# A prologue written out operation by operation: modulation quarters between the first projections

## The chip, the cores and the metric

One core of a Trainium2 chip runs the kernel; all its work is one program on five engines: TensorE (PE, its weight loads PEld), VectorE (DVE), ScalarE (ACT), GpSimd (POOL) and SyncE (SP, which issues loads). Each engine works through its own list of instructions in the order in which the program was written, and waits at an instruction until what it needs is there. The metric is the device time of one execution in microseconds (us), as the median over several runs.

## What is computed

Two layers of a backbone; each layer modulates and normalises its 1024 latent and 256 context tokens, projects them with `w_in`, mixes three groups of heads, gates and projects back. The prologue of layer 0, which the change rewrites, is this part of the reference (x stands for latent, ctx for context tokens):

```python
shift, scale, gate = jnp.split(jax.nn.silu(c) @ w_mod + b_mod, 3, axis=-1)
shift_c, scale_c, gate_c = jnp.split(jax.nn.silu(c_ctx) @ w_mod + b_mod, 3, axis=-1)
h = rms_norm(x, norm_g) * (1 + scale[:, None]) + shift[:, None]
hc = rms_norm(ctx, norm_g) * (1 + scale_c) + shift_c
p = h @ w_in          # layer 0 also: pc = hc @ w_in
```

## The kernel before, in words

Everything is float32. A projection takes three matmuls in place of one: the modulated activations and the weights are each split into a high half (rounded to the type that the fast matmul takes) and a low half (the rest), and high by high, low by high and high by low are added up in PSUM.

In the prologue of layer 0 these pieces occur:

- **Modulation quarters** q = 0 to 3. Shift and scale for the 1024 features are computed by quarters of 256 features; a quarter's weights are four loads of 512 KB (`mod0_load`). `mod0_mm` multiplies them on PE (8 matmuls, 16 records in the trace since each float32 matmul is two). `mod0_fin` turns the two result rows into columns: DVE copies them (L162), PE transposes four pieces (L166), and `mod_finish` makes shift and scale of them on DVE (L136 to L141). Quarter q serves the feature blocks k = 2q and 2q + 1.
- **Token tiles** j = 0 to 9, 128 tokens each: 0 to 3 are group g = 0, 4 to 7 are g = 1, the context tiles 8 and 9 are g = 2. A tile is loaded (L256), squared and summed on ACT in two halves (L266), its factor is computed on POOL (L267 to L269), and DVE multiplies the tile by it (L575).
- **A block (k, g)**, `h_block`: PE transposes feature block k of the group's tiles (L280), DVE (L286) or ACT (L284) applies scale and shift, ACT makes the high half (L287), POOL makes the low half, for g = 2 DVE (L289).
- **Gate matmuls** of (k, g): `proj_T_k` (L340), six matmuls on the block's two halves, for two column tiles of the first `w_in` chunk, which `w_split` has split (L317, L318).

Before, the order is this: loads of quarters 0 to 2, of the first `w_in` chunk, of all ten tiles, then of quarter 3 and the next chunk. PE computes quarters 0, 1 and 2 one after another. Then a loop goes over `items`: blocks k = 0 to 5 of g = 0, of g = 1, of g = 2, then the blocks of k = 6 and 7; the gate matmuls of an item come three items behind its block. Quarter 3 isn't computed on PE but on DVE: `mod0_acc` adds up 32 products (L176, L178) between items 8 and 15, and `mod0_sum` sums them over partitions with 16 small matmuls (L187). SP keeps a number of loads in flight and issues the next as an earlier one arrives. Behind the prologue come the Fourier matrices (L384) and the next projections.

Of the kernel before, what the change touches and what calls it, by code (L numbers as in the profile page):

```python
# [31 lines left out]
def build(tc, I, out):  # L32
# [127 lines left out]
    def mod0_fin(q, pm):  # L160
        row = E2()
        dve.tensor_copy(row[0:2, :], pm[0:2, :])  # L162
        ps = PX()
# [109 lines left out]
    def h_block(l, k, g, xn, H, on_act=False):  # L273
        tiles = GROUPS[g]
        s = 1 if g == 2 else 0
        n = 128 * len(tiles)
        c0 = tiles[0] * 128
        ps = PX()
        for i, j in enumerate(tiles):
            pe.transpose(ps[:, i * 128:i * 128 + 128], xn[j][:, k * 128:k * 128 + 128], ident)  # L280
# [251 lines left out]
    def layer(l, src, dst, carry):  # L532
# [27 lines left out]
        if full:  # L560
# [31 lines left out]
            W = wready.pop(0)  # L592
            a3 = T5([128, 4, 256])
            psg = [[PX() for _ in cols(ntokA)] for _ in range(2)]
            items = [(k, g) for g in (0, 1, 2) for k in range(6)] + [(k, g) for k in (6, 7) for g in (0, 1, 2)]
            at = {n: [] for n in range(len(items))}
            at[0] += [lambda: rms(0, 1, 2, 3), lambda: norm(0, 1), lambda: mod0_fin(2, ms[2]), lambda: norm(2, 3)]
            for n, j in enumerate((4, 5, 6, 7, 8, 9)):
                at[n] += [lambda j=j: rms(j)]
                at[n + 1] += [lambda j=j: norm(j)]  # L600
            for n in range(8, 16):
                at[n] += [lambda: next(acc)]
            at[18] += [lambda: mod0_sum(3, a3)]
            for n in range(len(items) + 3):
                if n < len(items):
                    for f in at[n]:
                        f()
                    hb(*items[n], 6 <= n < 17)
                if n == 0:
                    w3 = mod0_load(3)  # L610
                    acc = mod0_acc(w3, a3)
                    w_dma()
                if n >= 3:
                    gk(*items[n - 3])
                if n == 20:
                    dve.tensor_copy(identR, ident)
                    pool.tensor_scalar(pscT, pscT, 0.5, 0.0, MULT, ADD)
                    tabs = fourier_tabs(l)
                    css = [fourier_load(l, ct) for ct in range(2)]
                if n == 22:  # L620
                    w_split()
                    w_dma()
# [729 lines left out]
```

## Time and profile before

| | us |
|---|---|
| median of 3 runs | 1448.14 |
| lowest, highest | 1446.84, 1451.79 |
| the profiled execution's own time | 1448.99 |
| its span, first to last instruction | 1447.0 |
| PE busy | 1381.8 (95%) |
| DVE busy | 979.2 (68%) |
| POOL busy | 775.9 (54%) |
| ACT busy | 567.6 (39%) |

The profile is of one execution. An engine's busy share is a mean over stages that have different limits; what a rewritten prologue is worth is read from the prologue's own stretch, by when PE leaves it, and from whether PE has idle time behind it.

### The profile page before, as it was taken

To read this page: it belongs to the slowest core of one execution; us is meant where nothing else is said; L and a number is where in the kernel's file an instruction comes from. 1 tells how busy PE (TensorE), PEld (TensorE's weight loads), DVE (VectorE), ACT (ScalarE), POOL (GpSimd) and SP (SyncE) were. 2 spreads that over 40 slices of the span, in tenths; PEclk is the share of its full clock that TensorE was granted. 3 is DMA by queue.
4 is the path that set the end of the run, shared out by engine and by line. 5 is a ranking of instruction groups with operands and counts; after the bars stand their busy time and mean duration, and the time that the engine had idled before them with its cause. 6 is when DMAs were issued, how large, how long until landed. Compare 5 with 4: busy or idle time off the path is not lost.

```text
span 1447.0 us, 24063 instructions
## 1 busy us (share of the span) xinstructions
PE 1381.8 (95%) x9364; PEld 1240.6 (86%) x9364; DVE 979.2 (68%) x1553; ACT 567.6 (39%) x1230; POOL 775.9 (54%) x827
## 2 busy tenths in 40 slices
PE   7899999899999998999999899999999999999998
PEld 1688899779999987888888778988999998888887
DVE  2853366886895178798898654573464319989896
ACT  2632212101232265666665433121131227656663
POOL 2543222456785057667677842226887107766664
PEclk9899999999999999999999999999999999999999
DMA  9220242575123032112113321526412202111110
GB/s 354 101 90 32 85 149 91 187 266 166 60 88 117 1 103 81 66 45 74 45 45 112 104 66 38 205 80 213 148 44 85 78 22 67 45 45 45 59 59 30
DMA packets 65153, 137.07 MB, mean 95 GB/s; under 512 B 7312, under 2 KB 19728, under 8 KB 65040
## 3 DMA queue, kind: packets, MB, share of 16 engines
q1 hardware_dynamic: 49712, 108.82, 22.5%
q10 hardware_dynamic: 15328, 26.72, 5.3%
q8 instruction: 74, 1.21, 0.3%
q14 instruction: 39, 0.32, 0.1%
HBM read 105.63 MB, written 29.88 MB: 94 GB/s over the span
## 4 chain that ended last, share of the span: by engine, by line
PE 46%; DVE 21%; POOL 7%; issue 3%; ACT 2%; DMA 2%; ACTq 0%; POOLq 0%; SPq 0%; DVEq 0%
PE x L360 16%; DVE sm L923 6%; PE S L913 6%; PE x L1056 6%; PE x L993 5%; PE x L340 5%; PE x L753 3%; DVE e L1020 3%; PE x L977 2%; DVE t L952 1%; DVE t L980 1%; POOL e L759 1%; POOL sm L803 1%; DVE t L210 1%; PE x L892 1%
## 5 line engine op out<-in xcount | busy, mean ns | idle before, releaser
L360 PE MATMUL x<-wh,t 128*128 128x256 f32 x2432 | 445.9, 285 | 0.1
L360 PEld LDWEIGHTS x<-wh,t 128*128 128x128 f32 x2432 | 381.7, 192 | 1.8 <-issue 1.0
L360 PE MATMUL x<-wl,t 128*128 128x256 f32 x1216 | 344.7, 283 | 0.0
L923 DVE TENSOR_REDUCE sm<-S 128x1 f32<-128x1280 f32 (+1 forms) x132 | 194.8, 1476 | 72.2 <-PE S L913 72.0
L360 PEld LDWEIGHTS x<-wl,t 128*128 128x128 f32 x1216 | 233.7, 192 | 1.3 <-issue 1.2
L913 PE MATMUL S<-t,e 128*128 128x512 f32 (+1 forms) x768 | 180.9, 371 | 2.8 <-ACT e L899 1.4
L340 PE MATMUL x<-t,wh 128*128 128x512 f32 (+1 forms) x640 | 173.3, 381 | 8.8 <-DVE t L289 4.3
L938 ACT ACTIVATE t<-S,sm 128x1280 f32<-128x1280 f32 (+1 forms) x140 | 171.7, 1230 | 1.2 <-DVE sm L923 1.2
L993 PE MATMUL x<-t,t 128*128 128x128 f32 x1312 | 157.5, 275 | 3.3 <-DVE t L980 2.7
L993 PEld LDWEIGHTS x<-t,t 128*128 128x128 f32 x1312 | 153.7, 192 | 6.4 <-DVE t L980 2.9
L913 PEld LDWEIGHTS S<-t,e 128*128 128x128 f32 x768 | 126.3, 190 | 20.6 <-ACT t L938 2.0
L340 PEld LDWEIGHTS x<-t,wh 128*128 128x128 f32 x640 | 114.1, 192 | 31.6 <-POOL t L289 5.4
L318 POOL TENSOR_TENSOR wl<-st,wh 128x1024 fp32r<-128x1024 f32 x36 | 93.1, 2587 | 84.3 <-ACT wh L317 83.6
L961 POOL TENSOR_TENSOR t<-t,t 128x768 f32<-128x768 f32 (+1 forms) x64 | 116.2, 1816 | 5.3
L317 ACT ACTIVATE wh<-st 128x1024 fp32r<-128x1024 f32 x64 | 64.8, 1059 | 138.4 <-DMA xpart<-e 45.8
L977 PE MATMUL x<-ident,t 128*128 128x128 f32 x636 | 101.2, 274 | 5.7 <-DVE e L1059 4.1
L953 POOL TENSOR_SCALAR t<-t,sm 128x768 f32<-128x768 f32 x62 | 83.4, 1344 | 42.8 <-DVE sm L949 26.6
L753 PE MATMUL x<-wh,t 128*128 128x512 f32 x288 | 93.6, 404 | 8.5 <-DVE t L528 4.7
L1056 PE MATMUL x<-wh,e 128*128 128x512 f32 (+1 forms) x312 | 98.9, 384 | 2.6 <-ACT e L899 1.0
L340 PE MATMUL x<-t,wl 128*128 128x512 f32 (+1 forms) x320 | 100.2, 374 | 0.0
L210 DVE SCALAR_TENSOR_TENSOR t<-t,sc,t 128x512 f32<-128x512 f32 x98 | 90.8, 968 | 1.5 <-DMA t<-in_wmB_dram 1.1
L977 PEld LDWEIGHTS x<-ident,t 128*128 128x128 f32 x636 | 75.1, 141 | 15.9 <-DVE e L1059 4.5
(224 smaller groups left out, 2318.0 us busy)
## 6 DMA issues: line engine op xcount, KB each, us to landing
st<-in_w_in_dram SPq DMA_DIRECT2D x48, 512.0 KB, 4.0
t<-in_wmB_dram ACTq DMA_DIRECT2D x24, 512.0 KB, 5.4
xpart<-e ACTq DMA_DIRECT2D x36, 256.0 KB, 3.8
t<-xpart SPq DMA_DIRECT2D x18, 512.0 KB, 3.9
t<-in_wmS_dram SPq DMA_DIRECT2D x16, 512.0 KB, 8.5
st<-in_w_out_dram SPq DMA_DIRECT2D x16, 512.0 KB, 5.1
t<-in_x_dram SPq DMA_DIRECT2D x10, 512.0 KB, 10.3
e<-in_x_dram SPq DMA_DIRECT2D x20, 256.0 KB, 4.5
```

The lines of the kernel that those rows point to most:

```text
L210: dve.scalar_tensor_tensor(a, w, sk, a, MULT, ADD)
L318: lo_eng[hf].tensor_tensor(lo[:, sl, :], st, hi[:, sl, :].bitcast(F32), SUB)
L340: pe.matmul(p[:, :m], lhsT=W[wi][:, k, ct * 128:ct * 128 + 128], rhs=H[k][hi][:, c0:c0 + m], start=(n == 0), stop=(n == 3 * KT - 1))
L360: pe.matmul(bank[:, i * 256:i * 256 + 256], lhsT=H[k][hi][:, j * 128:j * 128 + 128], rhs=W[wi][:, k, :], start=(n == 0), stop=(n == 3 * KT ...
L753: pe.matmul(ps, lhsT=zr[k][zi][:, j * 128:j * 128 + 128], rhs=W[wi][:, k, :], start=(n == 0), stop=(n == 11))
L913: pe.matmul(S[:, i * nk + c:i * nk + c + n], lhsT=s["qT"][i][:, m * 2 + f, :], rhs=kT[2 * h + m][:, k0 + c:k0 + c + n], start=(f == 0), st ...
L923: dve.tensor_reduce(nb, S[:, :nh * nk].rearrange("p (h k) -> p h k", h=nh), AX.X, ALU.min)
L938: act.activation(p[:, sl], S[:, sl], AF.Exp, bias=nb[:, i:i + 1], scale=-1.0, accum_out=ls[:, i:i + 1])
L961: pool.tensor_tensor(p[0][:, cut:end], p[0][:, cut:end], p[1][:, cut:end], ADD)
L977: pe.transpose(ps[:, i * 128:i * 128 + 128], s["p"][0][:, (t0 + i) * 128:(t0 + i + 1) * 128], ident)
L993: pe.matmul(o[:, i * 128:i * 128 + 128], lhsT=s["PT"][:, i * nkt + t, :], rhs=vv[h][:, kt0 + t, :], start=(t == 0), stop=(t == nkt - 1))
L1056: pe.matmul(ps[:, :m], lhsT=zz[:, k, :], rhs=Wa[hf][wi][:, k, w0:w0 + m], start=(n == 0), stop=(n == 11))
```

## The change

The loop over items is replaced by a written list of operations: `m` computes a quarter on PE, `f` turns it, `n` squares, sums and multiplies a tile, `t` transposes a block, `s` splits it, `g` does its gate matmuls. All four quarters are computed on PE; `mod0_acc` and `mod0_sum` are gone. `h_block` is cut in two, `h_trans` and `h_split`. The two small operations of a tile's factor move from POOL to DVE, its power stays on POOL. The loads come in the order quarter 0, x0 to x3, the chunk of `w_in`, quarter 1, x4 to x7, quarter 2, x8 and x9, quarter 3. The context's gate matmuls (`g02` to `g72`) all come last.

```diff
-    def mod0_acc(ws, acc):
-        for k in range(KT):
-            for i in range(2):
...
-    def mod0_sum(q, acc):
...
+    def h_trans(k, g, xn):
+        ps = PX()
+        for i, j in enumerate(GROUPS[g]):
+            pe.transpose(ps[:, i * 128:i * 128 + 128], xn[j][:, k * 128:k * 128 + 128], ident)
+        return ps
...
             def rms(*js):
                 for j in js:
                     rx[j] = SM(1)
-                    for _ in x_rms(xn[j], rx[j]):
-                        pass
+                    ss = SM(2)
+                    for hf in range(2):
+                        sq = E2()
+                        act.activation(sq, xn[j][:, hf * 512:hf * 512 + 512], AF.Square, accum_out=ss[:, hf:hf + 1])
+                    dve.tensor_tensor(rx[j], ss[:, 0:1], ss[:, 1:2], ADD)
+                    dve.tensor_scalar(rx[j], rx[j], 1.0 / D, EPS, MULT, ADD)
+                    pool.tensor_tensor(rx[j], rx[j], mhalf[:, 0:1], ALU.pow)
...
+            def run(op, *a):
+                if op == "m":
+                    mods[a[0]] = mod0_mm(wm[a[0]])
+                elif op == "f":
+                    mod0_fin(a[0], mods[a[0]])
+                elif op == "n":
+                    rms(*a)
+                    norm(*a)
+                elif op == "t":
+                    banks[a] = h_trans(*a, xn)
+                elif op == "s":
+                    newH(a[0])
+                    h_split(l, *a, banks[a], H, a[0] >= 4 and a[1] == 1)
+                elif op == "g":
...
+            wm = [mod0_load(0)]
+            x_in(0, 1, 2, 3)
             w_dma()
-            x_in(0, 1, 2, 3, 4, 5, 6, 7, 8, 9)
-            ms = [mod0_mm(wm[0])]
-            ms.append(mod0_mm(wm[1], lambda: mod0_fin(0, ms[0])))
-            ms.append(mod0_mm(wm[2], lambda: mod0_fin(1, ms[1])))
-            w_split()
...
+            wm.append(mod0_load(1))
+            x_in(4, 5, 6, 7)
+            wm.append(mod0_load(2))
+            x_in(8, 9)
+            wm.append(mod0_load(3))
+
+            for text in (
+                    "m0 n0 n1 f0 n2 n3 t00 t10 s00 t20 s10 W t30 m1 g00 f1 g10 s20 s30 n4 n5 n6 n7 g20 g30",
+                    "t01 t11 s01 t21 s11 t31 s21 g01 s31 g11 m2 g21 f2 g31 t40 t50 s40 n8 n9 t41 s50 t51 s41 g40 s51 g50",
+                    "t02 t12 s02 g41 s12 g51 t22 t32 s22 s32 m3 t42 f3 t52 s42 s52 X t60 t70 s60 s70 t61 s61 g60",
+                    "t71 s71 g70 Y t62 t72 g61 s62 s72 g71 g02 g12 g22 g32 g42 g52 g62 g72"):
```

`W` splits the first chunk of weights and issues the next, `X` makes small constants and issues the Fourier tables' loads, `Y` splits the second chunk. Behind the prologue the order of the instructions is the same on every engine.

What the list does to the engines' queues shows at three places. The first is PE's queue around the first transposes of token tiles (tiles `t_17` and on, into `x_297`). Before (x_200 is quarter 2's result, L166 the turning):

```order
L157 MATMUL x_200<-t_12_140,sc 2x512 x2
L166 MATMUL x_207<-ident,e_33_205 128x2 x4
L157 MATMUL x_200<-t_13_142,sc 2x512 x2
L157 MATMUL x_200<-t_14_144,sc 2x512 x2
L166 MATMUL x_274<-ident,e_61_272 128x2 x4
L280 MATMUL x_297<-ident,t_17_150 128x128
```

and after, where quarter 1 (into `x_281`) follows the last transposes of group 0 (block 3, into `x_276`), and the first gate matmuls (into `x_290`) follow it:

```order
L252 MATMUL x_276<-ident,t_9_134 128x128
L252 MATMUL x_276<-ident,t_10_136 128x128
L155 MATMUL x_281<-t_13_142,sc 2x512 x2
L155 MATMUL x_281<-t_14_144,sc 2x512 x2
L155 MATMUL x_281<-t_15_146,sc 2x512 x2
L155 MATMUL x_281<-t_16_148,sc 2x512 x2
L321 MATMUL x_290<-t_53_249,wh_266 128x512
L321 MATMUL x_290<-t_54_250,wh_266 128x512
L321 MATMUL x_290<-t_53_249,wl_267 128x512
```

Quarters 1 to 3, of which two stood ahead of every transpose of a tile, now stand between them.

The second place is ACT's queue at the squares of the tiles of group 1. Before, the squares (L266, of `t_21` and `t_22`, tiles 4 and 5) stand around the high half of block (0, 0), `t_68`:

```order
L266 ACTIVATE e_59_263,sm_262<-t_20_156 128x512
L266 ACTIVATE e_60_265,sm_262<-t_20_156 128x512
L266 ACTIVATE e_66_288,sm_287<-t_21_158 128x512
L266 ACTIVATE e_67_290,sm_287<-t_21_158 128x512
L287 ACTIVATE t_68_295<-e_71_302 128x512
L266 ACTIVATE e_80_321,sm_320<-t_22_160 128x512
```

and after, the tiles 4 and 5 are `t_17` and `t_18`, and `t_71` and `t_74` are the high halves of blocks (2, 0) and (3, 0), which use quarter 1:

```order
L298 ACTIVATE wh_266<-st_140 128x1024
L265 ACTIVATE t_71_316<-e_73_318 128x512
L265 ACTIVATE t_74_322<-e_76_324 128x512
L554 ACTIVATE e_79_330,sm_329<-t_17_150 128x512
L554 ACTIVATE e_80_332,sm_329<-t_17_150 128x512
L554 ACTIVATE e_83_340,sm_339<-t_18_152 128x512
```

The squares of tiles 4 and on have moved behind four high halves and the split of the weights.

The third place is DVE's queue at the context tiles. Before, tiles 8 and 9 (`t_25`, `t_26`) are multiplied between the scalings (L286) of group 0, and the products of quarter 3 (L176) follow:

```order
L286 TENSOR_SCALAR e_109_404<-x_399,scaleT_99,shiftT_97 128x512
L575 TENSOR_SCALAR t_25_166<-t_25_166,sm_388 128x1024
L286 TENSOR_SCALAR e_117_431<-x_426,scaleT_99,shiftT_97 128x512
L575 TENSOR_SCALAR t_26_168<-t_26_168,sm_415 128x1024
L176 TENSOR_SCALAR t_38_227<-t_72_306,sc 128x256 x4
```

and after, they stand between the scalings of blocks (4, 0) and (5, 0) (`e_111`, `e_123`), behind the end of quarter 2 (L141):

```order
L141 TENSOR_TENSOR scaleT_99<-sm_453,ngT 128x4
L264 TENSOR_SCALAR e_111_475<-x_463,scaleT_99,shiftT_97 128x512
L555 TENSOR_TENSOR sm_479<-sm_480 128x1
L556 TENSOR_SCALAR sm_479<-sm_479 128x1
L561 TENSOR_SCALAR t_25_166<-t_25_166,sm_479 128x1024
L555 TENSOR_TENSOR sm_489<-sm_490 128x1
L556 TENSOR_SCALAR sm_489<-sm_489 128x1
L561 TENSOR_SCALAR t_26_168<-t_26_168,sm_489 128x1024
L264 TENSOR_SCALAR e_123_506<-x_468,scaleT_99,shiftT_97 128x512
```

The two tiles' six operations have moved in front of the scaling of block (5, 0); the products of quarter 3 are gone.

## Rows read from the trace of the kernel before

**Rows 1.** The page's head and its first part: busy time (share of the span) and instructions.

```profile
span 1447.0 us, 24063 instructions
PE 1381.8 (95%) x9364; PEld 1240.6 (86%) x9364; DVE 979.2 (68%) x1553; ACT 567.6 (39%) x1230; POOL 775.9 (54%) x827
```

**Rows 2.** Busy time of the engines in stretches of the prologue and behind it: from:to and length in us, then busy us (instructions) of PE, PEld, DVE, ACT, POOL, the granted clock as a share of 2.4 GHz, the DMA engines' busy share, GB/s.

```profile
0.00:15.60 15.60, 9.67 (x18) 1.77 (x19) 0.98 (x5) 1.70 (x3) 0.19 (x4) 1.00 0.85 286
15.60:38.10 22.50, 17.99 (x59) 6.28 (x58) 10.71 (x23) 9.90 (x26) 9.92 (x17) 0.91 1.04 404
38.10:64.40 26.30, 23.68 (x115) 18.23 (x113) 20.99 (x25) 19.39 (x41) 21.04 (x27) 0.94 0.24 89
64.40:72.20 7.80, 4.70 (x25) 4.16 (x23) 7.80 (x21) 1.96 (x4) 0.00 (x0) 0.75 0.25 70
72.20:92.40 20.20, 17.64 (x99) 15.78 (x98) 11.84 (x21) 7.01 (x18) 8.70 (x6) 0.84 0.33 106
92.40:250.00 157.60, 157.58 (x1005) 141.08 (x1006) 82.98 (x145) 37.55 (x67) 45.22 (x28) 1.00 0.25 83
```

**Rows 3.** PE's waits from 0 to 92 us: who waited for what, us in total, times, longest.

```profile
PE x L157 <- DMA t<-in_wmS_dram: 5.9, 1, 5.9
PE x L340 <- DVE t L289: 4.3, 3, 2.4
PE x L166 <- DVE e L162: 3.2, 1, 3.2
PE x L280 <- DVE t L575: 2.4, 3, 1.1
```

**Rows 4.** PE's timeline from 0 to 38.2 us: start, us, then line, operation, out<-in, shapes, count, and the idle time before with what ended it.

```profile
5.93 12.61 PE L157 MATMUL x<-t,sc 128*2 128x512 f32 x24 [5.93 <-DMA t<-in_wmS_dram]
18.47 0.40 PE L166 MATMUL x<-ident,e 2*128 2x2 f32 x4
18.80 7.03 PE L157 MATMUL x<-t,sc 128*2 128x512 f32 x16
...
26.10 3.60 PE L157 MATMUL x<-t,sc 128*2 128x512 f32 x8
32.92 0.41 PE L166 MATMUL x<-ident,e 2*128 2x2 f32 x4 [3.23 <-DVE e L162]
...
35.45 3.04 PE L280 MATMUL x<-ident,t 128*128 128x128 f32 x13 [0.18 <-DVE t L575]
38.14 1.50 PE L340 MATMUL x<-t,wh 128*128 128x512 f32 x2
```

**Rows 5.** PE's timeline, the starts of two items of latent tiles in a row, of a context item and of the item behind it, and the prologue's end.

```profile
41.09 0.60 PE L280 MATMUL x<-ident,t 128*128 128x128 f32 x4
...
42.92 0.60 PE L280 MATMUL x<-ident,t 128*128 128x128 f32 x4
...
83.84 0.38 PE L280 MATMUL x<-ident,t 128*128 128x128 f32 x2
...
84.77 0.63 PE L340 MATMUL x<-t,wh 128*128 128x512 f32 x2
...
90.42 1.06 PE L384 MATMUL x<-e 128*128 128x128 f32 x8
```

**Rows 6.** SP's timeline: the issues of the ten tile loads.

```profile
15.14 12.21 SPq L256 DMA_DIRECT2D t<-in_x_dram  x10
```

**Rows 7.** ACT's timeline: the squares of tile 0 and the start of tile 1.

```profile
25.75 0.63 ACT L266 ACTIVATE e<-t 128x512 f32<-128x512 f32 x1 [0.23 <-DMA t<-in_x_dram]
...
27.04 0.63 ACT L266 ACTIVATE e<-t 128x512 f32<-128x512 f32 x1
```

**Rows 8.** DVE's timeline (and one row of POOL's): the copy of quarter 0, its four small operations, POOL's power for tile 0 and DVE's multiplication of that tile.

```profile
15.15 0.68 DVE L162 COPY e<-x 2x512 f32<-2x512 f32 x1 [11.78 <-PE x L157]
18.91 0.16 DVE L136 TENSOR_TENSOR shiftT<-x,bmodT 128x4 f32<-128x4 f32 x1 [3.09 <-PE x L166]
18.99 0.15 DVE L139 TENSOR_TENSOR sm<-x,bmodT 128x4 f32<-128x4 f32 x1
19.18 0.17 DVE L140 TENSOR_SCALAR sm<-sm 128x4 f32<-128x4 f32 x1
19.38 0.16 DVE L141 TENSOR_TENSOR scaleT<-sm,ngT 128x4 f32<-128x4 f32 x1
...
29.46 0.56 POOL L269 TENSOR_TENSOR sm<-sm,mhalf 128x1 f32<-128x1 f32 x1
...
30.05 0.75 DVE L575 TENSOR_SCALAR t<-t,sm 128x1024 f32<-128x1024 f32 x1 [0.72 <-POOL sm L269]
```

**Rows 9.** The split of block (0, 0) on DVE, ACT and POOL.

```profile
35.97 0.81 DVE L286 TENSOR_SCALAR e<-x,scaleT,shiftT 128x512 f32<-128x512 f32 x1 [0.57 <-PE x L280]
...
36.81 0.63 ACT L287 ACTIVATE t<-e 128x512 fp32r<-128x512 f32 x1 [4.54 <-DVE e L286]
...
37.52 1.27 POOL L289 TENSOR_TENSOR t<-e,t 128x512 fp32r<-128x512 f32 x1 [1.72 <-ACT t L287]
```

**Rows 10.** Groups of instructions from 0 to 90.4 us: line, engine, operation, names, shapes, count, then busy us, mean ns of one, idle before.

```profile
L178 DVE SCALAR_TENSOR_TENSOR t<-t,sc,t 128x256 f32<-128x256 f32 x28 | 13.5, 543 | 0.0
...
L187 PE MATMUL x<-ones,t 128*128 128x1 f32 x16 | 3.4, 343 | 0.0
...
L176 DVE TENSOR_SCALAR t<-t,sc 128x256 f32<-128x256 f32 x4 | 5.3, 1376 | 0.0
```

**Rows 11.** Busy time in stretches that follow the granted clock, columns as in rows 2. No clock is on record yet in the first stretch, where 1.00 stands.

```profile
5.90:10.20 4.30, 4.27 (x6) 0.67 (x7) 0.00 (x0) 0.00 (x0) 0.00 (x0) 1.00 0.98 308
10.20:15.50 5.30, 5.30 (x14) 1.10 (x13) 0.35 (x1) 0.00 (x0) 0.00 (x0) 1.00 1.02 371
30.00:33.00 3.00, 0.08 (x1) 0.08 (x2) 2.09 (x3) 2.25 (x8) 2.65 (x8) 1.00 1.03 410
34.20:41.00 6.80, 6.03 (x20) 4.87 (x21) 4.50 (x6) 3.60 (x10) 4.75 (x7) 0.50 1.04 393
64.40:68.30 3.90, 1.51 (x12) 1.14 (x9) 3.90 (x11) 0.98 (x2) 0.00 (x0) 1.00 0.03 9
68.30:78.50 10.20, 9.48 (x45) 9.32 (x45) 7.12 (x20) 2.03 (x4) 0.29 (x1) 0.50 0.50 146
78.50:90.40 11.90, 10.26 (x61) 8.60 (x61) 8.13 (x9) 4.63 (x7) 8.42 (x6) 1.00 0.19 62
```

More of the change, by code (lines that the diff above doesn't have):

```diff
@@ L150, in mod0_load, with mod0_mm @@
         return ws
-    def mod0_mm(ws, half_way=None):
+    def mod0_mm(ws):
         ps = PX()
         for k in range(KT):
-            if k == KT // 2 and half_way:
-                half_way()
             pe.matmul(ps[0:2, :], lhsT=sc[:, k, :], rhs=ws[k // 2][:, k % 2, :], start=(k == 0), stop=(k == KT - 1))
@@ L271, in build, with h_split @@
     GROUPS = {0: (0, 1, 2, 3), 1: (4, 5, 6, 7), 2: (8, 9)}
-    def h_block(l, k, g, xn, H, on_act=False):
-        tiles = GROUPS[g]
-        s = 1 if g == 2 else 0
[L276 to L280, printed above, removed]
+    def h_trans(k, g, xn):
[3 more added lines that the diff above has]
+        return ps
+    def h_split(l, k, g, ps, H, on_act=False):
+        s = 1 if g == 2 else 0
+        n = 128 * len(GROUPS[g])
+        c0 = GROUPS[g][0] * 128
         hf = E2()
@@ L289, in h_block @@
         eng.tensor_tensor(H[k][1][:, c0:c0 + n], hf[:, :n], H[k][0][:, c0:c0 + n].bitcast(F32), SUB)
+    def h_block(l, k, g, xn, H, on_act=False):
+        h_split(l, k, g, h_trans(k, g, xn), H, on_act)
     wsrc = []
@@ L590, in layer @@
-            ms.append(mod0_mm(wm[2], lambda: mod0_fin(1, ms[1])))
-            w_split()
[L592 to L622, printed above, removed]
+            psg = [[None] * len(cols(ntokA)) for _ in range(2)]
@@ new lines, in layer @@
+            banks, mods = {}, {}
+            def run(op, *a):
[12 more added lines that the diff above has]
+                elif op == "g":
+                    k, g = a
+                    for ct in range(2):
+                        if psg[ct][g] is None:
+                            psg[ct][g] = PX()
+                        proj_T_k(psg[ct], H, W, ct, ntokA, k, (g,))
@@ new lines, in layer @@
+            wm = [mod0_load(0)]
+            x_in(0, 1, 2, 3)
+            w_dma()
+            wm.append(mod0_load(1))
[4 more added lines that the diff above has]
+            for text in (
[4 rows of a table added]
+                for op in text.split():
+                    if op == "W":
+                        w_split()
+                        W = wready.pop(0)
+                        w_dma()
+                    elif op == "X":
+                        dve.tensor_copy(identR, ident)
+                        pool.tensor_scalar(pscT, pscT, 0.5, 0.0, MULT, ADD)
+                        tabs = fourier_tabs(l)
+                        css = [fourier_load(l, ct) for ct in range(2)]
+                    elif op == "Y":
+                        w_split()
+                        w_dma()
+                    else:
+                        run(op[0], *map(int, op[1:]))
```

23 lines of the change are left out of this document (removed).

## The prediction

> **What bounds the kernel now.** First the page: PE is busy 95% of a span of 1447.0 us [rows 1], so whatever holds PE up is paid for at the end, unless PE has slack later. Then the busy time by stretches [rows 2]. The prologue ends for PE at 90.4, where the last gate matmul is followed by L384 [rows 5]. From 92.4 to 250 PE is busy 157.58 of 157.60 us: no slack there that could swallow a later start, and the order of all instructions behind the prologue is the same in both kernels. So the question is when the prologue ends. The view of PE's waits says what it loses now [rows 3]: 5.9 for the first load, 3.2 for DVE's copy of the third modulation quarter, 2.4 for normalised tiles, 4.3 for DVE's low halves. The timeline of PE [rows 4] shows the order: PE does three modulation quarters one behind another (5.93 to 29.7), nearly all of it while the latent tiles are still being loaded (the first one arrives at 25.75 [rows 7]). The first gate matmul comes at 38.14.
>
> **The loads.** SP's queue holds 512 KB loads, and issues one as an earlier one arrives: ten x loads are issued in 12.21 us [rows 6], 1.3 each, and the loads arrive at that pace. The 15th load (x0) arrives at 25.7 [rows 7], so the 5th at about 12.5. In the changed kernel the 5th to 8th are x0 to x3 (12.5 to 16.4), the w_in chunk follows (19), quarter 1 (24.2), x4 to x7 (29.4), quarter 2 (34.6), x8 and x9 (37.2), quarter 3 (42.4). All these are estimates from those two rows.
>
> **PE's work behind quarter 0.** Quarter 0 ends at about 15.5 in both kernels (DVE's copy starts at 15.15 [rows 8]). A quarter is 16 matmul records; 16 take 7.0 us [rows 4], 6.9 without the last one's tail. A latent item (four transposes, six gate matmuls) takes 42.92 - 41.09 = 1.83, a context item 84.77 - 83.84 = 0.93 [rows 5]. A quarter's turning (f) takes 0.4 [rows 4]. After the change: three quarters 20.7, four f 1.6, 16 latent items 29.3, 8 context items 7.4: 59.0. If PE never waited and the clock stayed at 2.4 GHz, the prologue would end at 15.5 + 59.0 = 74.5, 16 us earlier than now. What it waits must be added.
>
> **The steps that hold PE up.** The chain of a split: DVE 0.81, ACT 0.63, POOL 1.27, with hand-overs 2.8 us from DVE's start to the low half, 1.5 to the high half [rows 9]. Turning a quarter: copy 0.68, PE 0.4, four small DVE operations 0.65 [rows 4, 8]. Normalising a tile: ACT's two squares 1.29 [rows 7], then on DVE two small operations (0.15, 0.17), POOL's power 0.56, DVE's 0.75 [rows 8]. DVE's queue holds the next tile's small operations behind this tile's multiplication, so tiles follow each other at 1.7 us with the hand-overs.
> (a) DVE has x0 and x1 ahead of quarter 0's copy: x0 ready at 15.7, x1 at 17.4; copy and f until 18.5, then x2 and x3 at 20.9 and 22.6. PE, done with quarter 0 at 15.5, waits 2.5 and then 3.9: 6.4.
> (b) t00 to t30 and quarter 1 follow (22.6 to 33.6, with the slow clock below). Blocks k = 2, 3 need quarter 1: g00, f1, g10 run to 36.6, s20 starts on DVE at 36.1 and its low half is there at 38.9. PE waits 2.1, and finishes g30 at 41.5.
> (c) The squares of x4 to x7 stand on ACT behind the high half of s30 (38.2), which waited for quarter 1, though the tiles have been there since 29.4. x4 is normalised at 41.9, x7 at 47.0. PE waits 5.1 for t01. Behind these squares nobody else waits.
> (d) g01, g11, quarter 2 (to 60.4), g21, f2, g31 and four transposes fill PE until 65.2. s40 needs quarter 2 and starts at 64.2: low half at 67.0, PE waits 1.5. On DVE the normalisation of x8 and x9 stands between s40 and s50, and their squares stand on ACT behind s40's high half (65.6): x9 is done at 70.5, s50's high half at 71.9, its low half at 73.3. PE waits 4.6 at g50.
> (e) Quarter 3 fills PE from 81 to 88. s60 stands on DVE behind f3 and s42, s52, whose DVE, ACT, DVE chains take 1.35 each: it starts at 92.7, its low half is there at 95.6. PE waits 0.9 and 4.5: 5.4.
> Sum of the waits: 6.4 + 2.1 + 5.1 + 6.1 + 5.4 = 25.1. The move of the row sums' two small operations from POOL to DVE costs DVE 0.3 a tile, within the 1.7. The removed work (32 accumulations on DVE, 13.5 + 5.3 us, and 16 summing matmuls, 3.4 [rows 10]) stood in PE's way only by DVE's late low halves, the 4.3 of [rows 3], and by the clock.
>
> **The clock.** After PE has stood nearly still from 30 to 33 the granted clock is 0.50 from 34.2 to 41.0, the 1.2 GHz level, and again from 68.3 to 78.5 after the waits of 64.4 to 68.3 [rows 11]; in the first of these 13 transposes take 38.14 - 35.45 = 2.7 [rows 4], 0.21 each, twice their time. From 78.5 to 90.4, where PE is idle for 1.6 us in pieces, it stays at 1.00. Waits (a), (c), (d) and (e) are of that size. The slow stretches last 6.8 and 10.2 us, and at the start of the kernel six matmuls take 4.27 us, then 14 take 5.30 [rows 11]. I charge half speed to the first 3 to 6 us of work behind each, nearest to the shortest of these: 14 transposes and 3 quarter-matmuls (2.8), 14 transposes and 3 gate matmuls (2.2), g50 to g41 (3.0), g60 to g70 (1.6): 9.6. Its bounds: nothing (the clock never falls), and 16.5, where quarter 2 also runs at half speed (6.9 more). [...]
>
> **The sum.** 74.5 + 25.1 + 9.6 = 109.2. Before's prologue, added up in the same way from the same durations, comes out at 93.1 where the trace has 90.4; I compare sum with sum: 109.2 - 93.1 = 16 us later. A check by the work left: when g30 ends (41.5) the changed kernel still has two quarters, two f and 29.4 of items before it, 44 us, so it would end at 85.5 without another wait: it may lose 4.9 us more to break even, and (c) alone is 5.1. The profiled execution took 1448.99 (the table of times), so 1465; the median is 0.85 lower, which changes nothing at this precision. A difference of 0.3%, 4.3 us, is about what a measurement of this kernel can tell from no change.
>
> **The rivals.** *The clock stays up* (the transposes between the waits keep it at 2.4 GHz): the 9.6 go, and before's stays as it was, +6: 1455. *The clock falls for a whole quarter*: +16 + 6.9 = +23: 1472. *DVE's relief decides* (the other side): DVE was busy 7.80 of 7.80 us from 64.4 to 72.2 [rows 2], its first four accumulations took 1.38 each beside POOL's low halves, against 0.54 for the others [rows 10]; without them POOL and DVE never hold each other up, every split arrives while PE is in a quarter, and waits (c) to (e) fall away with their clock: 109.2 - 16.6 - 6.8 = 85.8, 7 us under before's sum: 1442. It decides once less than 4.9 us are lost after 41.5. For it speak the 1.38, and that DVE then has idle time of up to 10 us during quarter 2; against it, that the idle time lies before the instructions that wait for the quarter, and no engine takes them earlier out of its queue. [...] *Half of it* (c and e hidden, d not): waits 10.5 and clock 3.8 less than the sum, +2: 1451, no difference to be told. *Given back later*: PE waits little until 250 [rows 2], and all later loads are issued by instructions that shift along with it; I count it with the half case.
>
> **How the numbers follow.** The main case (+9 to +22, 1458 to 1471) 0.67; the falling clock beyond that (+22 to +30) 0.07; the flat clock, or one of (c) to (e) hidden (+4.3 to +9) 0.11; the half case 0.08; DVE's relief 0.07. Slower by over 0.3% 0.85, within 0.3% 0.08, faster 0.07. The range leaves out the relief, the half case and the top beyond +24 (0.05): 1453 to 1473. The likeliest one is 1465.
>
> **What would show it.** Right: the first gate matmul at 33 to 35, earlier than 38.14; PE waiting some 5 us for the normalisation of x7 near 42 to 47, 4 to 5 us for s50 near 70 and for s60 near 92; a granted clock of 0.50 behind them; L384's successor at 104 to 111 instead of 90.4, and the same 157 us of unbroken work behind it. Wrong: quarter 1 to 3 shorter than 6.9 each; squares of x4 to x7 finished before 38; or a prologue that ends late with a span that does not.

## The result, and the profile after

The changed kernel takes 1467.31 us (median of four runs, 1463.40 to 1470.75), the kernel before 1449.66 in the same comparison: 1.0122 times as long, 95% interval 1.0089 to 1.0156. It is slower by about 18 us, and 1465 with a range from 1453 to 1473 had been predicted. The profiled execution took 1466.14. The page's head and its first part, beside [rows 1]:

```profile
span 1464.3 us, 24043 instructions
PE 1390.5 (95%) x9368; PEld 1238.7 (85%) x9368; DVE 964.6 (66%) x1549; ACT 563.7 (38%) x1223; POOL 768.8 (52%) x807
```

PE's busy time has grown by 8.7 us, that of the other engines has shrunk: these shares say nothing of a loss of 17.3 us in the span. PE's timeline does. Its rows with idle time from 0 to 109 us, and those of quarter 1 and of the first gate matmul (columns as in [rows 4]; L155 is a quarter, L164 its turning, L252 a transpose of a tile, L321 a gate matmul, L365 the Fourier matrices, which were L384), and the last one as against [rows 5]:

```profile
5.05 9.63 PE L155 MATMUL x<-t,sc 128*2 128x512 f32 x16 [5.05 <-DMA t<-in_wmS_dram]
17.11 0.58 PE L164 MATMUL x<-ident,e 2*128 2x2 f32 x4 [2.43 <-DVE e L160]
...
20.09 0.47 PE L252 MATMUL x<-ident,t 128*128 128x128 f32 x1 [1.78 <-DVE t L561]
21.77 3.04 PE L252 MATMUL x<-ident,t 128*128 128x128 f32 x13 [1.20 <-DVE t L561]
24.73 8.33 PE L155 MATMUL x<-t,sc 128*2 128x512 f32 x16
32.99 0.73 PE L321 MATMUL x<-t,wh 128*128 128x512 f32 x2
...
37.29 0.50 PE L321 MATMUL x<-t,wh 128*128 128x512 f32 x1 [0.70 <-ACT t L265]
38.65 0.50 PE L321 MATMUL x<-t,wh 128*128 128x512 f32 x1 [0.85 <-POOL t L267]
...
41.61 0.30 PE L252 MATMUL x<-ident,t 128*128 128x128 f32 x1 [0.17 <-DVE sm L555]
43.21 0.33 PE L252 MATMUL x<-ident,t 128*128 128x128 f32 x1 [1.29 <-DVE t L561]
44.88 0.47 PE L252 MATMUL x<-ident,t 128*128 128x128 f32 x1 [1.34 <-DVE t L561]
46.55 3.03 PE L252 MATMUL x<-ident,t 128*128 128x128 f32 x13 [1.20 <-DVE t L561]
...
65.79 0.50 PE L321 MATMUL x<-t,wh 128*128 128x512 f32 x1 [0.26 <-ACT t L265]
67.14 0.50 PE L321 MATMUL x<-t,wh 128*128 128x512 f32 x1 [0.85 <-POOL t L267]
...
71.88 0.80 PE L321 MATMUL x<-t,wh 128*128 128x512 f32 x1 [3.30 <-ACT t L265]
73.23 0.80 PE L321 MATMUL x<-t,wh 128*128 128x512 f32 x1 [0.56 <-POOL t L267]
...
88.53 0.40 PE L164 MATMUL x<-ident,e 2*128 2x2 f32 x4 [0.40 <-DVE e L160]
...
93.90 0.50 PE L321 MATMUL x<-t,wh 128*128 128x512 f32 x1 [3.13 <-ACT t L265]
95.25 0.50 PE L321 MATMUL x<-t,wh 128*128 128x512 f32 x1 [0.85 <-POOL t L267]
...
108.87 1.06 PE L365 MATMUL x<-e 128*128 128x128 f32 x8
```

The first gate matmul starts at 32.99, five us earlier than before. That isn't five us gained: at this point PE still has two quarters before it (14 us), where the kernel before had only the 16 sums of quarter 3 (3.4 in [rows 10]). Then come the waits at t01 (41.6 to 46.6), g40 and g50 (65.8 to 73.2) and g60 (93.9, 95.3), and L365 starts at 108.87, where L384 started at 90.42: 18.45 later. Behind it hardly anything comes back: of the next 157.6 us PE is busy 157.52, as before ([rows 2], last row), and the whole rest of the span is 1355.4 us against 1356.6, less apart than other kernels are (last section). Busy time in stretches, columns as in [rows 2]: four that follow the granted clock (to be compared with [rows 11]), quarter 2, and the work behind the prologue:

```profile
17.15:27.39 10.24, 7.26 (x24) 4.03 (x25) 5.93 (x13) 3.15 (x4) 4.41 (x5) 0.50 1.04 398
44.46:51.29 6.83, 5.21 (x18) 4.28 (x19) 4.58 (x8) 2.52 (x4) 3.22 (x4) 0.50 0.01 4
71.77:78.59 6.82, 6.16 (x16) 4.58 (x17) 1.43 (x4) 3.49 (x7) 4.00 (x4) 0.50 0.27 77
95.66:99.07 3.41, 3.41 (x12) 2.73 (x11) 0.00 (x0) 1.67 (x3) 2.05 (x2) 0.50 0.00 0
53.20:60.20 7.00, 7.00 (x17) 1.27 (x16) 0.00 (x0) 0.00 (x0) 0.43 (x1) 1.00 0.00 0
110.80:268.40 157.60, 157.52 (x1004) 140.99 (x1005) 82.81 (x146) 37.62 (x68) 45.14 (x28) 1.00 0.25 83
```

The granted clock falls to 0.50 at four places in the prologue: at the waits for f0 and t00 (17.1 to 21.8), at those for t01, at g50 and behind g60. It falls at no other; for the very start no clock is on record, and quarter 0's 16 matmul records take 9.63 there, against 7.03 for quarter 2's. The row of quarter 2 is the other half of the story: for 7 us PE works alone, DVE and ACT have not one instruction, although the context tiles had arrived by 36.6. What could have been done then is done later, while PE waits.

### The profile page after: what moved, and what is told of

Same layout as the page of the kernel before. It is cut to its first block, busy times and chain, and to the rows that moved or that the text cites. A ratio compares the mean times of both kernels' runs of the same rounds, so it can differ in the third digit from the quotient of the medians.

```text
span 1464.3 us, 24043 instructions
## 1 busy us (share of the span) xinstructions
PE 1390.5 (95%) x9368; PEld 1238.7 (85%) x9368; DVE 964.6 (66%) x1549; ACT 563.7 (38%) x1223; POOL 768.8 (52%) x807
## 4 chain that ended last, share of the span: by engine, by line
PE 46%; DVE 21%; POOL 6%; DMA 3%; issue 3%; ACT 2%; ACTq 0%; POOLq 0%; SPq 0%; DVEq 0%
PE x L341 16%; DVE sm L916 6%; PE S L906 6%; PE x L1049 6%; PE x L986 5%; PE x L321 5%; PE x L746 4%; DVE e L1013 3%; PE x L970 2%; DVE t L945 1%; DVE t L973 1%; POOL sm L796 1%; DMA xpart<-e 1%; PE x L885 1%; POOL wl L299 1%
## 5 line engine op out<-in xcount | busy, mean ns | idle before, releaser
L321 PE MATMUL x<-t,wh 128*128 128x512 f32 (+1 forms) x640 | 172.5, 381 | 13.1 <-ACT t L265 7.4
L321 PEld LDWEIGHTS x<-t,wh 128*128 128x128 f32 x640 | 114.3, 192 | 39.0 <-ACT t L265 9.0
L298 ACT ACTIVATE wh<-st 128x1024 fp32r<-128x1024 f32 x64 | 64.7, 1059 | 117.3 <-DVE t L186 38.2
L321 PE MATMUL x<-t,wl 128*128 128x512 f32 (+1 forms) x320 | 100.4, 375 | 0.0
```

Source lines behind the costliest of these rows:

```text
L321: pe.matmul(p[:, :m], lhsT=W[wi][:, k, ct * 128:ct * 128 + 128], rhs=H[k][hi][:, c0:c0 + m], start=(n == 0), stop=(n == 3 * KT - 1))
```

## The experiments

Every experiment but e6 starts from the changed kernel; each makes one edit, but e4 joins three of them, and b2 and b4 write the list anew. The time of the first load (5.05 to 5.81) and the length of the first stretch of half speed (6.8 or 10.2 us) differ from execution to execution for the same first instructions, so the start of g20 (37.29 in the changed kernel) moves by up to 1.4 down and 1.0 up. The table therefore gives, beside the prologue's end (start of L365 or what stands for it), the time from g20's first matmul to it, both from the profiled execution, and the median time. Each trace is of one execution.

| kernel | g20 starts | prologue ends | from g20 to the end | against the changed one | median us |
|---|---|---|---|---|---|
| before | | 90.42 | | | 1449.7 |
| changed | 37.29 | 108.87 | 71.58 | | 1467.3 |
| e1, squares of x4 to x7 early | 37.85 | 109.48 | 71.63 | 0 | 1467.7 |
| e8, squares, sums and power early | 35.90 | 103.21 | 67.31 | -4.3 | 1465.1 |
| e1b, n4 and n5 early | 36.90 | 104.51 | 67.61 | -4.0 | 1465.0 |
| e2, n8 and n9 early | 36.31 | 100.05 | 63.74 | -7.8 | 1460.6 |
| e3, s60 and s70 first | 36.45 | 103.55 | 67.10 | -4.5 | 1463.9 |
| e7, context's gates into the wait | 38.28 | 107.35 | 69.07 | -2.5 | 1468.1 |
| e4, three places together | 36.02 | 92.44 | 56.42 | -15.2 | 1451.3 |
| e5, idle PE filled | 34.55 | 101.32 | 66.77 | -4.8 | 1462.3 |
| e6, before with quarter 3 on PE | | 91.93 | | | 1450.5 |
| b2, another list | | 81.99 | | | 1441.6 |
| b4, another list and loads | | 81.94 | | | 1442.8 |

Not all of these differences are the edits'. e2 and e3 gain 0.6 and 0.3 between g20 and g40, ahead of what they alter, and e8 gains 0.6 behind g40, since the stretches of half speed fall differently over the same work. Counted only where the edit stands (from g20 to g40, or from g40 to the end), the gains are 3.7 for e8, 4.1 for e1b, 7.3 for e2 and 4.2 for e3. In the median time e1b and e8 are only 2.3 and 2.2 us faster than the changed kernel, within the spread of its runs, so for these two the reading rests on the traces.

**The wait at t01: ACT, or POOL?** The first edit moves the squares alone (`q` is a new operation that does only them):

```
-"... W t30 m1 g00 f1 ..."
+"... W t30 q4 q5 q6 q7 m1 g00 f1 ..."
```

> The changed kernel with one edit: the squares of x4 to x7 on ACT stand ahead of quarter 1 instead of behind the high half of block (3, 0). Everything else of these tiles (sums, power, multiplication) stays where it is. The prediction's step (c) names ACT's squares as what PE waits for: if so, DVE has x4 to x7 one after another at 1.7 us from 37.5 on, x7 is done at 43.5 to 44.5 instead of 46.5, PE's wait for t01 shrinks from 4.0 to 1 to 2 us, and the prologue ends 2.5 to 4 us earlier: 105 to 106.5 instead of 108.9, 1464. Rival: the tiles' power stands on POOL behind the low halves of blocks (2, 0) and (3, 0), which end at 39.8 and 41.0, so x4 can't be done before 41.6 whatever ACT does: PE's waits at t01 stay 4.0, the end stays 108.9 +-0.5, 1467.

Nothing was won: 109.48, 1467.72 us, 1.0122 (1.0088 to 1.0156) of before. The squares were done by 31.7, yet the multiplications (L568) came when they came before. DVE's and POOL's timelines of this kernel say why (L562 and L563 are the sums, L564 the power, L267 the low halves of blocks (2, 0) and (3, 0)):

```profile
37.95 0.15 DVE L563 TENSOR_SCALAR sm<-sm 128x1 f32<-128x1 f32 x1
40.93 0.75 DVE L568 TENSOR_SCALAR t<-t,sm 128x1024 f32<-128x1024 f32 x1 [2.82 <-POOL sm L564]
...
42.61 0.75 DVE L568 TENSOR_SCALAR t<-t,sm 128x1024 f32<-128x1024 f32 x1 [0.67 <-POOL sm L564]
```
```profile
37.87 2.51 POOL L267 TENSOR_TENSOR t<-e,t 128x512 fp32r<-128x512 f32 x2 [7.91 <-ACT t L265]
40.34 0.55 POOL L564 TENSOR_TENSOR sm<-sm,mhalf 128x1 f32<-128x1 f32 x1
42.02 0.56 POOL L564 TENSOR_TENSOR sm<-sm,mhalf 128x1 f32<-128x1 f32 x1 [1.12 <-DVE sm L563]
```

x4's sums are done at 38.1; DVE then stands still for 2.82, because the power of x4 is third in POOL's queue, behind two low halves that take 2.51. After that each tile takes about 1.7: DVE waits 0.67 for a power, and POOL 1.12 for the next tile's sums, which stand on DVE behind this tile's multiplication. POOL took these three in the order of the list: the power starts at 40.34, as the second low half ends, 2.2 behind its sums. Two more edits take that chain away, in part and as a whole:

```
e1b: -"... t30 m1 g00 f1 g10 s20 s30 n4 n5 n6 n7 ..."
     +"... t30 n4 n5 m1 g00 f1 g10 s20 s30 n6 n7 ..."
e8:  +"... t30 r4 r5 r6 r7 m1 ..."   (r: squares, sums and power; n4 to n7 multiply only)
```

> The changed kernel with one edit: n4 and n5, whole (squares, sums, power, multiplication), stand ahead of quarter 1; n6 and n7 stay behind s20 and s30. After the squares alone moved nothing (the prologue still ended at 109.5), two theories are left for the 4.0 us that PE waits at t01. POOL's queue: the power of x4 and x5 now stands ahead of the low halves of blocks (2, 0) and (3, 0), so only x6 and x7 have to wait behind these (41.6 and 43.3 instead of 44.9 and 46.5): PE waits 1 to 2 us at t01, the prologue ends 2.5 to 4.5 us earlier, 104.5 to 106.5 instead of 108.9, 1463 to 1465. PE's or DVE's own pace (DVE's multiplications for x4 and x5 then hold up the copy of quarter 1, and what is gained at t01 is lost at f1): 108 to 109.5, 1467.

> The changed kernel with one edit: for x4 to x7 the squares on ACT, the sums on DVE and the power on POOL stand ahead of quarter 1; only the four multiplications on DVE stay behind s20 and s30. With the squares alone early nothing was won: DVE had the sums of x4 done at 38.1, and the power started at 40.34, when POOL was through with the low halves of blocks (2, 0) and (3, 0); then each tile took 1.67, its power behind its sums and its sums behind the last tile's multiplication. If that chain over DVE and POOL is what PE waits for at t01, the four multiplications now follow each other from 37.5 on, none is later than 42, PE waits under 0.5 there in place of 4.0, some of it given back at g20 and g30 by low halves that lock with the multiplications (1 us), and the prologue ends at 104 to 106.5 instead of 108.9, 1463 to 1465. If PE waits for something else there, its wait stays at 3 to 4 us and the end at 108 to 109.5, 1467.

Both came out as the chain over DVE and POOL has it: 104.51 (1464.98) and 103.21 (1465.10). The second is 0.8 earlier than its range, with g20 1.4 earlier than in the changed kernel. In e8 PE's timeline goes from the low half of block (2, 0) straight to g01, with no wait at t01 left:

```profile
37.73 0.50 PE L321 MATMUL x<-t,wh 128*128 128x512 f32 x1 [1.33 <-POOL t L267]
...
44.13 0.49 PE L321 MATMUL x<-t,wh 128*128 128x512 f32 x1 [0.26 <-ACT t L265]
```

The low half there is 0.5 later than in the changed kernel (1.33 in place of 0.85), with the multiplications beside it. That part of the expectation, 1 us, was too dear: this 0.5 is all that e8 shows of low halves that lock with multiplications.

**The wait at g50.**

```
-"... m2 g21 f2 g31 t40 t50 s40 n8 n9 t41 s50 ..."
+"... m2 n8 n9 g21 f2 g31 t40 t50 s40 t41 s50 ..."
```

> The changed kernel with one edit: n8 and n9 (squares, sums, power and multiplication of the context tiles) stand right behind quarter 2 in the list, ahead of the scaling of block (4, 0), instead of between the scalings of blocks (4, 0) and (5, 0). They then run while PE is in quarter 2. By step (d) the 3.3 and 0.6 us that PE waits at g50 go, and with them the stretch of half speed behind them: the prologue ends 5 to 8 us earlier, at 101 to 104 instead of 108.9, 1459 to 1462. If block (5, 0) were late for another reason (ACT's queue, or POOL and DVE holding each other up), the wait would stay, the end 108 to 109, 1467.

The wait is gone, and the clock stays up behind its place: 100.05, 1460.61 us, 7.8 less behind g20, of which 7.3 behind g40. The end is 1 us earlier than its range, and g20 starts 1.0 earlier than in the changed kernel. PE's next idle time behind g40 is that of the turning of quarter 3 (beside 71.88 and 73.23 above):

```profile
65.57 0.50 PE L321 MATMUL x<-t,wh 128*128 128x512 f32 x1 [0.84 <-POOL t L267]
...
79.74 0.40 PE L164 MATMUL x<-ident,e 2*128 2x2 f32 x4 [0.40 <-DVE e L160]
```

**The wait at g60**, first on DVE's side, then on PE's:

```
e3: -"... f3 t52 s42 s52 X t60 t70 s60 s70 ..."
    +"... f3 t52 t60 t70 s60 s70 s42 s52 X ..."
e7: -"... s61 g60 ... s72 g71 g02 g12 g22 g32 g42 ..."
    +"... s61 g02 g12 g22 g32 g60 ... s72 g71 g42 ..."
```

> The changed kernel with one edit: t60, t70, s60, s70 stand ahead of s42, s52 and X instead of behind them. By step (e) block (6, 0) is split 2.7 us earlier (two DVE, ACT, DVE chains of 1.35 each), PE's waits at g60 shrink from 4.0 to 1 to 1.5 us, and the prologue ends 2.5 to 5 us earlier: 104 to 106.5 instead of 108.9, 1462.5 to 1465. If the wait at g60 came from the turning of quarter 3 alone, it would stay: 108 to 109, 1467.

> The changed kernel with one edit, on PE alone: the context's gate matmuls of blocks 0 to 3 (g02 to g32, 24 of the 48 that the change puts last) stand ahead of g60, whose data PE waits for, instead of at the end. Their halves are done by then. If the 4.0 us that PE waits at g60 are a wait for one block while other work is ready, as step (e) has it, these 2.9 us of work go into it and the clock stays up behind it: the prologue ends 2 to 4 us earlier, 105 to 107 instead of 108.9, 1463.5 to 1465.5. If they only move the wait (the context's halves late too, or the banks taken), it ends at 108 to 109.5, 1467.

e3 ends at 103.55, 1463.91 us: 5.3 earlier, a little more than expected, with g20 0.8 earlier; 4.5 less behind g20, 4.2 behind g40. e7 missed. PE's timeline of e7 where the context's gate matmuls now stand:

```profile
92.41 0.47 PE L321 MATMUL x<-t,wh 128*128 128x256 f32 x2 [0.80 <-DVE e L264]
94.09 0.51 PE L321 MATMUL x<-t,wh 128*128 128x256 f32 x2 [1.08 <-DVE e L264]
```

They wait 1.88 for a scaling on DVE (L264), whose result they don't use; what they most likely wait for is the PSUM bank that it reads. That was not tried by itself, but the filler kernel e5 below agrees: at the same place its 24 transposes, which read nothing but the identity, wait for the same scaling (L273 there):

```profile
85.48 2.84 PE L254 MATMUL x<-ident 128*128 128x128 f32 x24 [0.71 <-DVE e L273]
```

In e7, about half of the 4.0 at g60 is won, the clock does not fall there, and the end comes 2.5 earlier from g20. The median, 1468.09, does not show it. In this profiled execution the span is 1468.3, so 1361.0 lie behind the prologue, against 1355.4 in the changed kernel, and PE is busy 157.44 of the next 157.6 us all the same. Whether e7 gains anything in time is left open.

**All three places.** e1b, e2 and e3 in one list:

> The changed kernel with all three places of its list altered: n4 and n5 ahead of quarter 1, n8 and n9 behind quarter 2, and t60, t70, s60, s70 ahead of s42. The quarters stay between the projections on PE, the loads as in the changed kernel. If the loss is that of these three places, as steps (c) to (e) have it, their gains add up: 8.8 and 5.3 as measured one by one, and 2.5 to 4.5 for n4 and n5, 16.6 to 18.6: the prologue ends at 90.5 to 93 (before 90.4), 1449 to 1452, no difference to the kernel before. If the loss lies in what the list does as a whole (quarters on PE between short bursts, the clock, the loads' order), the three overlap, and it ends at 96 to 100, 1456 to 1460.

92.44, 1451.30 us, 1.0012 (0.9998 to 1.0027) of before: nearly the whole loss is back, with every quarter still on PE. From g20 on, the three gains of 4.0, 7.8 and 4.5 make 16.3 (15.5 where the edits stand), and together they gave 15.2. So they add up, and the list's idea as a whole costs little: 2.0 us against before.

**The clock.** In e5, 120 transposes of the identity matrix are put where PE is idle:

```
+def pad(n):
+    ps = PX()
+    for _ in range(n):
+        pe.transpose(ps[:, 0:128], ident, ident)
 ahead of f0: 20; of the transposes of x2 and x3 in t00: 14, 9; of x5, x6, x7 in t01: 9 each; of g50: 26; of g60: 24
```

> The changed kernel with idle PE filled: transposes of the identity matrix into a spare bank, which nobody reads, stand in PE's list where it waits: 20 ahead of f0, 14 and 9 ahead of the third and fourth transpose of t00, 9 ahead of each of the last three of t01, 26 ahead of g50, 24 ahead of g60. At 0.107 us each they are shorter than the waits at these places. The data chains are unchanged. By the prediction's term for the clock (9.6 us, bounds 0 and 16.5) the granted clock stays at 1.00 and the prologue ends 7 to 10 us earlier although PE has 13 us more to do: 99 to 102 instead of 108.9, 1457 to 1460. If the clock costs nothing, since PE would only wait longer for the same data, the end stays at 107 to 110, 1466 to 1468.

The end comes at 101.32, 7.55 earlier, within its range, although PE has more to do. The time, 1462.27 us, is 2.3 above its range; in the profiled execution 1359.6 us lie behind the prologue, against 1355.4 in the changed kernel. The granted clock stays at 1.00 from 10.8 on:

```profile
10.80:101.30 90.50, 81.50 (x418) 50.68 (x417) 36.36 (x81) 32.62 (x72) 31.84 (x29) 1.00 0.47 174
```

and PE's timeline gives the price of each fall, by the lead over the changed kernel at the same matmul (here g20, x7's transpose, g40, g50, f3; line numbers differ from the changed kernel's):

```profile
34.55 0.50 PE L330 MATMUL x<-t,wh 128*128 128x512 f32 x1 [0.70 <-ACT t L274]
...
43.80 1.64 PE L261 MATMUL x<-ident,t 128*128 128x128 f32 x13 [0.36 <-DVE t L570]
...
62.31 0.51 PE L330 MATMUL x<-t,wh 128*128 128x512 f32 x1 [0.26 <-ACT t L274]
...
68.39 0.50 PE L330 MATMUL x<-t,wh 128*128 128x512 f32 x1 [0.46 <-ACT t L274]
...
82.54 0.40 PE L164 MATMUL x<-ident,e 2*128 2x2 f32 x4 [0.40 <-DVE e L160]
...
101.32 1.06 PE L374 MATMUL x<-e 128*128 128x128 f32 x8
```

The lead is 2.74 at g20, 2.75 at x7, 3.48 at g40, 3.49 at g50, 5.99 at f3 and 7.55 at the end. So the falls behind (a), (c), (d) and (e) cost 2.7, 0.7, 2.5 and 1.6. The first price is that of this execution, with 10.24 us of half speed; e2, whose first stretch lasted 6.8, is only 1.8 behind e5 at g20. At these four places the clock was at 0.50 behind waits of 4.0 to 5.4 us together, and at 1.00 in e5, where transposes fill most of them. At (b) it goes either way. In the changed kernel waits of 0.70 and 0.85 left the clock at 1.00; in e2, with nothing altered up to there, the same two waits were followed by 3.4 us of half speed:

```profile
36.31 0.50 PE L321 MATMUL x<-t,wh 128*128 128x512 f32 x1 [0.69 <-ACT t L265]
37.66 0.50 PE L321 MATMUL x<-t,wh 128*128 128x512 f32 x1 [0.85 <-POOL t L267]
```
```profile
38.58:41.99 3.41, 3.41 (x10) 2.34 (x8) 2.01 (x6) 3.29 (x12) 1.39 (x3) 0.50 1.05 393
```

e8 has such a fall there too, behind waits of 0.64 and 1.33. In e2 it cost nothing, since x7's transpose comes 9.25 behind g20 in it and 9.26 in the changed kernel: PE would have waited for the tiles. So the length of a wait alone doesn't tell whether the clock falls.

**DVE's relief alone.** In the kernel before, quarter 3 goes to PE and all else stays:

```
...
-for n in range(8, 16):
-    at[n] += [lambda: next(acc)]
-at[18] += [lambda: mod0_sum(3, a3)]
+at[14] += [lambda: ms.append(mod0_mm(w3))]
+at[18] += [lambda: mod0_fin(3, ms[3])]
```

> The kernel before with quarter 3 on PE: its 8 matmuls stand ahead of item 14, its turning ahead of item 18 where the 16 summing matmuls stood; DVE's 32 products are gone. All else is as before, loads and order too. This is the relief of DVE by itself. By the prediction's main case the products cost PE only the waits for the low halves (4.3) and the clock behind them (about 3), against 7.0 - 3.4 more work on PE and one turning: -3 to +1, the prologue ends at 87.5 to 91.5 instead of 90.4, 1446 to 1451. By the rival that DVE's relief decides, POOL and DVE no longer hold each other up and the gain is 6 us or more: 84.5 or earlier, 1443.

91.93, 1450.54 us, 1.0001 (0.9988 to 1.0014) of before, a little over what was expected and far from the rival's 84.5. The same 7.8 us as in [rows 2], in which DVE was busy all the time and PE 4.70, and the stretch of half speed behind them, which lasted 10.20 in [rows 11]:

```profile
64.40:72.20 7.80, 7.80 (x27) 2.97 (x26) 0.43 (x1) 1.18 (x3) 0.00 (x0) 1.00 0.10 28
77.15:80.57 3.42, 3.42 (x17) 3.42 (x18) 1.62 (x6) 0.63 (x1) 0.85 (x1) 0.50 0.50 143
```

Now it is PE that is busy for 7.80, with the quarter (until 69.9) and the items behind it, and DVE for 0.43. The products had held up DVE's low halves, and PE with them. Taking them away puts a quarter on PE, 7 us, and a turning with a wait of 1.8 for its copy; it saves the 16 sums (3.4), 3.1 of waits for low halves and two thirds of this half speed. The balance is an end 1.5 us later and no difference in time. That DVE and POOL hold each other up, as the prediction's rival has it, may well be in the 1.38 of [rows 10]; that row and the 0.54 beside it are of two different operations, so they don't show it alone. One operation in both positions is the multiplication of a tile in the kernel before: 0.75 at 30.05 [rows 8], and 1.77 at 51.37, beside a run of POOL's low halves. That DVE is held up beside POOL is likely, but taking the products away won nothing here.

**A list without these waits.** With the rules that the first experiments suggested (a tile is squared, summed and multiplied as soon as it is there; what PE needs next is split several operations ahead; gate matmuls come well behind their splits), the list was written anew. It differs in many places at once, so it shows what an order can reach and not what each place is worth. Its first half in b2:

```
"m0 n0 n2 f0 m1 W n3 n1 t30 t50 n4 f1 m2 n5 t00 t40 t20 n7 n6 s30 f2 n9 t01 n8",
"s50 s00 t10 m3 t51 t41 s10 s51 s01 f3 t31 t22 t71 s20 s40 t32 s22 s41 g00 t70 t21 s70 g10 s31",
```

> The changed kernel with another list, loads and all other code the same: each tile's squares and multiplication stand as soon as its load has come (n4 to n9 by the end of quarters 1 and 2), quarters 1, 2 and 3 stand closer together between transposes of tiles that have come, and every gate matmul comes eight or more operations behind its split. If order in the queues is what the changed kernel loses by, and not its quarters on PE, PE waits under 2 us behind the second turning, the clock stays at 1.00 there, and the prologue ends at 80 to 84, 7 to 10 us earlier than in the kernel before: 1439 to 1443. If POOL (its low halves, 1.3 each) or the loads set the pace instead, it ends at 86 to 90, 1446 to 1450.

> A third list with another order of loads: quarter 0, x8 and x9, x0 to x3, quarter 1, x4 to x7, quarter 2, the first w_in chunk, quarter 3; tiles and blocks in the order in which these come. In the other new list (prologue to 82.0, 1441.6) PE waits 3.7 for the turning of quarter 0 and 1.3 for loads, and never after 31; what is left is the loads' pace. If so, this list can gain little: it ends at 80 to 83, 1439 to 1443. If a later w_in chunk makes gate matmuls wait in the end, 84 to 87, 1444 to 1447.

b2: 81.99, 1441.55 us, 0.9929 of before (0.9913 to 0.9946); b4: 81.94, 1442.79 us, 0.9959 (0.9943 to 0.9975). Both beat both kernels. The rows of b2 in which PE has idle time, all that there are from 15 us to its prologue's end, and a stretch of windows:

```profile
18.84 0.58 PE L164 MATMUL x<-ident,e 2*128 2x2 f32 x4 [3.71 <-DVE e L160]
20.43 8.84 PE L155 MATMUL x<-t,sc 128*2 128x512 f32 x16 [1.00 <-DMA t<-in_wmS_dram]
...
30.95 7.03 PE L155 MATMUL x<-t,sc 128*2 128x512 f32 x16 [0.33 <-DMA t<-in_wmS_dram]
...
81.99 1.06 PE L365 MATMUL x<-e 128*128 128x128 f32 x8
```
```profile
38.00:82.00 44.00, 44.00 (x241) 33.37 (x242) 24.07 (x45) 19.13 (x37) 24.56 (x20) 1.00 0.35 121
```

Behind quarter 2's start at 30.95 PE never waits; from 38 on it is busy 44.00 of 44.00 at a granted clock of 1.00. What is left lies ahead of that, with the loads, the first turning and one stretch of half speed, from about 17 to 24, in which quarter 1 begins: it takes 8.84, against 7.03 for quarter 2.

## Why the prediction was right, and where its reasons were not

**The end and the sum.** 1465 was predicted, 1466.1 profiled and 1467.3 measured; 109.2 for the prologue, 108.87 in the trace. That the sum of 109.2 is so near is in part luck, since its errors cancel. The forecast of time came from the difference of two sums, +16; the trace has +18.45 for the prologue and +17.3 for the span. Waits: 25.1 predicted, 20.3 in the timeline above (5.41 in (a), 1.55 in (b), 4.00 in (c), 4.97 in (d), 4.38 in (e)), each of them smaller. The clock: 9.6 predicted, 7.55 by e5. The two terms are not independent, and the prediction took them so. In the four slow stretches PE was busy for 22.0 us, of which 11.0 are the half speed's; 3.5 of these fall where PE would have waited for data otherwise, which shortens the waits. So 74.5 + 20.3 + 11.0 = 105.8. That leaves 3 us, or 4 from where quarter 0 really ended (14.68, where the prediction had 15.5). They are likely the matmuls ahead of the sixteen waits, which count with their whole 0.27 to 0.50 us where in a row the next one starts after 0.11 to 0.23; that is worked out, not tested. The prediction's sum for before had gone wrong by 2.7 in the other direction. The 2.4 and 1.2 GHz that the prediction names are in no view of a trace: these give the granted clock as a share of full speed, here 1.00 and 0.50.

**Step by step.** (a) right: 6.4 and 5.41, and its half speed 2.8 and 2.7. First gate matmul at 33 to 35: 32.99. (b) right: 2.1 and 1.55, with no fall of the clock in this execution; e2 and e8 show that it could have come. (c) right in place, 1.1 too dear in size (5.1 and 4.00; x7's transpose at 46.55 for 47.0), wrong in its cause. The failing sentence is that the squares of x4 to x7, late behind the high half of s30, are what PE waits for. They were late; but e1 had them done eleven us earlier (the last at 31.7 in place of 42.9) and won nothing, since x4's power was as late in POOL's queue. The prediction had looked past POOL there. The wait was that of two queues, nearly equal, then of a serial chain of 1.67 a tile, whose pace it had (1.7). The half speed behind (c) cost 0.7, not 2.2: in e5, at full speed, PE waits 0.25 and 0.86 for g01's splits instead. The check by the work left (4.9 us to lose behind 41.5) holds too: 13.4 of waits and 4.8 of half speed were lost there. (d) right in cause, 1.1 too dear: 6.1 and 4.97, half speed 3.0 and 2.5; e2 took both away. (e) right in cause, 1.0 too dear: 5.4 and 4.38, half speed 1.6 and 1.6; e3 confirms that s42 and s52 ahead of s60 were the cause.

**The rivals.** DVE's relief did not decide: without the products the waits (c) to (e) are all there, 13.4 us, and e6 won nothing by it. The clock did not stay up, nor fall for a whole quarter: quarters 2 and 3 took 7.03 each, at full speed; only quarter 1 had some of it (8.33). Little if anything was given back later (157.52 of 157.60; 1355.4 us behind the prologue against 1356.6). The argument against the relief, that DVE's idle time lies ahead of the instructions that wait for a quarter and no engine takes them earlier, is what e2 shows from the other side: as soon as two tiles' work was written into that idle time, 7.8 us were won.

## What to carry to other kernels

Where engines work through written lists, a long piece on one of them (here 7 us of a quarter on PE) is free time on the others only if their work of that time stands ahead of whatever waits for the piece; go through each queue behind it and ask what is ready and stands behind something that is not. When one late instruction is moved and nothing changes, look at the next queue that the same value goes through: a squaring on ACT, sums on DVE, a power on POOL, and each of them can be the one that is behind. And waits on PE can cost more than themselves: here those of 4.0 to 5.4 us at a place cost another 0.7 to 2.7 us by half speed, least where PE, at full speed, would only have come to its next wait earlier.

## What had not been expected of the hardware

Transposes that nobody reads, put into PE's idle time, kept the granted clock at 1.00 and brought the end of the prologue from 108.87 to 101.32, with no data chain altered. The same two waits, 0.7 and 0.85 us long, left the clock at 1.00 in one kernel and were followed by 3.4 us at 0.50 in another (e2). The same first instructions of PE run with 6.8 us of half speed in some kernels (e1b, e2, e3) and 10.2 in others (the changed one, e7), and quarter 1, which starts near the stretch's end, takes 7.86, 7.03 and 7.63 in the first three, 8.33 and 8.16 in the other two: a difference of up to 1.7 us that no edit made. And the rest of the span behind the prologue, the same instructions in the same order, took 1355.4 to 1361.0 us from kernel to kernel, so a gain of a few us in the prologue is read from the trace and not from one span.
